# The linear attention's branch product: four dense products beside the gates, or two wide seven-product groups ahead of them

## The chip, the cores and the metric

One core of one Trainium2 chip runs the whole layer. The metric is the device time of one execution in microseconds (us), the median of three runs. A core has five engines that run their own instruction lists in order and wait for one another by semaphores: TensorE (PE in the profile; PEld is its weight load), VectorE (DVE), ScalarE (ACT), GpSimd (POOL) and SyncE (SP). In this kernel SP issues the loads from memory, and POOL issues transfers that add in flight and the writes of intermediate results.

## The reference

One decoder layer on 256 tokens of width 2048, all in float32. What matters here is the merge of three mixers:

```python
y_gla = (o_gla * jax.nn.silu(gr)) @ w_br_gla[l]      # (256, 1024) @ (1024, 2048)
y_sb  = stick_breaking_mixer(...) @ w_br_sb[l]
y_mem = memory_mixer(...) @ w_br_mem[l]
g = jax.nn.sigmoid(gates.reshape(B, T, N_BRANCH, D)) # gates = h @ W_in's last 6144 columns
merged = g[:, :, 0] * y_gla + g[:, :, 1] * y_sb + g[:, :, 2] * y_mem
x = x + merged @ w_o[l]
```

After it comes a SwiGLU feed-forward part. `y_gla` is the branch product of the title.

## The kernel before

Every weight matrix is read from memory once, in tiles `raw` of 128 partitions by 4 by 512 (1 MB): four blocks of 128 rows of the contraction and one block of 512 columns. TensorE multiplies pairs of numbers: each float32 operand is split into a high part (`wh`, made by ACT, L151) and a low part (`wl` = `raw` - `wh`, made by DVE, L152), and a product is three matmuls, high by high, high by low and low by high. The split goes in halves of 128x1024, two row blocks each. The tiles for `wh` and `wl` form a ring of five halves, so ACT and DVE can be at most five halves ahead of TensorE. A matmul has a 128x128 block of activations as weights and streams 512 columns into one PSUM bank; the 256 tokens are two blocks `t`.

There are two ways to multiply.

- `gemm` (L224 to L226): the dense product of one block of 512 columns, with two accumulators. Every half feeds 12 matmuls. The branch products and the first projections use it.
- `sgemm` (L269 to L272): two column blocks at once, a "wide group", in which part of the contraction goes by Winograd's form of Strassen's scheme, seven block products instead of eight. The blocks are two token blocks, two column blocks and two halves of the contraction, `p` row blocks long. The products are called p1 to p7 (L329 to L368: `p1`, `p2`, `p3`, `q4`, `p5`, `p6`, `p7`); a half of a product feeds 6 matmuls. p3, p5, p6 and p7 need sums of activations, the "forms" (tiles `s` before; `make_forms` makes them on DVE and ACT, L413). p5 and p6 need sums of weights: DVE adds `raw` tiles (L284). Two more sums of weights are made by transfers of POOL that add in flight (L332 and L352). What Strassen's scheme leaves over is multiplied densely by `rest`, 12 matmuls a half. DVE (L317) and ACT (L315, L346) move sums between PSUM banks and SBUF pieces `cv`. A product's second token block is added at its end by DVE (L409).

Small work such as transposes (L460), forms and merges is put in a list `background` of generators; `step()` runs one piece of it after each half, and `flush()` runs all. Behind the Python order stands a scheduler that moves instructions of each engine ahead by its own estimate, so the final order on each engine is not that of the code.

The part in question: the gates are 6144 columns, 2048 for each branch. A loop over `b` in (2, 1, 0) makes two wide groups for each branch. For `b` = 2 and 1 the sigmoid (ACT, L1078) is merged with the branch product in the background: for `b` = 1 the product was written to memory (`ysd`) and is read back as `yr`. Each merge of a column block and token block is a multiplication (L1057) and an addition (L1058). For `b` = 0, after each wide group of gates, two dense products with `w_br_gla` follow, and DVE takes them from PSUM (L1090, L1091). When four merged column blocks are there, they are transposed into chunks for the next product with `w_o`, whose forms are made during the last two dense products.

```python
        for n0 in range(0, D, 2 * NB):       # b == 0: two wide groups of gates
            ...
            if n0 > 0:
                sm_ = make_forms(tm[:1], form_tiles())
            for n, g in zip((n0, n0 + NB), gs):
                y = gemm(xo, a["w_br_gla"], n)
```

## Time and profile before

| | |
|---|---|
| time, median of 3 runs (lowest to highest) | 1609.48 us (1608.88 to 1610.42) |
| the profiled execution: time, span of its instructions | 1609.76 us, 1608.0 us |
| granted TensorE clock in it | 1.000 |
| instructions in the trace | 19432 |
| bytes moved by DMA | 395.76 MB, mean 246 GB/s |

The page gives, engine by engine, the time in which it was busy and its share of the span. A matmul's end is modelled and matmuls overlap in the records (one lasts about 0.39 us there, and the next starts sooner), so a busy TensorE says little by itself; the number of matmuls in a stretch says how fast it went.

In the profiled execution the two wide groups of gates for `b` = 1 end at about 701.2 us, and the next wide group begins there. From there to about 828.7 us stand the gates of `b` = 0 and the four dense products; the product with `w_o` follows.

### The profile page before, as it was taken

To read this page: it belongs to the slowest core of one execution; us is meant where nothing else is said; L and a number is where in the kernel's file an instruction comes from. 1 tells how busy PE (TensorE), PEld (TensorE's weight loads), DVE (VectorE), ACT (ScalarE), POOL (GpSimd) and SP (SyncE) were. 2 spreads that over 40 slices of the span, in tenths; PEclk is the share of its full clock that TensorE was granted. 3 is DMA by queue.
4 is the path that set the end of the run, shared out by engine and by line. 5 is a ranking of instruction groups with operands and counts; after the bars stand their busy time and mean duration, and the time that the engine had idled before them with its cause. 6 is when DMAs were issued, how large, how long until landed. Compare 5 with 4: busy or idle time off the path is not lost.

```text
span 1608.0 us, 19432 instructions
## 1 busy us (share of the span) xinstructions
PE 1600.8 (100%) x7198; PEld 1314.4 (82%) x7198; DVE 1361.7 (85%) x1555; ACT 1048.6 (65%) x1281; POOL 74.9 (5%) x97
## 2 busy tenths in 40 slices
PE   9999999999999999999999999999999999999998
PEld 7888888888788888888888888888888888888887
DVE  6788788887677788987799998988878989888996
ACT  7666677776666666665656766666666666666663
POOL 0000000000000000000000000000010000110000
PEclk9999999999999999999999999999999999999999
DMA  9766768667555888888757868777898686897694
GB/s 381 287 230 213 242 216 261 214 180 254 193 183 179 289 263 255 278 280 289 235 187 259 277 224 256 253 255 236 262 281 259 215 272 232 256 277 244 200 327 153
DMA packets 66672, 395.76 MB, mean 246 GB/s; under 512 B 7377, under 2 KB 14161, under 8 KB 21649
## 3 DMA queue, kind: packets, MB, share of 16 engines
q1 hardware_dynamic: 50928, 322.92, 52.5%
q0 software_dynamic: 12080, 68.16, 22.2%
q10 hardware_dynamic: 3568, 3.44, 0.7%
q8 instruction: 56, 0.92, 0.2%
q14 instruction: 40, 0.32, 0.1%
HBM read 324.24 MB, written 12.58 MB: 209 GB/s over the span
## 4 chain that ended last, share of the span: by engine, by line
PE 98%; DMA 1%; ACT 0%; DVE 0%; issue 0%; ACTq 0%; DVEq 0%
PE acc L269 20%; PE acc L272 20%; PE acc L271 20%; PE tmp L272 7%; PE tmp L269 7%; PE tmp L271 7%; PE acc L225 4%; PE acc L226 4%; PE acc L224 4%; PE tmp L460 2%; DMA raw<-in_w_br_mem 0%; PE tmp L701 0%; PE tmp L729 0%; DMA xraw<-in_memT 0%; PE tmp L817 0%; PE tmp L826 0%
## 5 line engine op out<-in xcount | busy, mean ns | idle before, releaser
L152 DVE TENSOR_TENSOR wl<-raw,wh 128x1024 fp32r<-128x1024 f32 (+1 forms) x768 | 923.9, 1222 | 204.3 <-ACT wh L151 190.3
L151 ACT CAST wh<-raw 128x1024 fp32r<-128x1024 f32 (+1 forms) x769 | 801.7, 1053 | 443.5 <-PE acc L272 238.7
L269 PE MATMUL acc<-wh,xTh 128*128 128x512 f32 x532 | 210.7, 396 | 0.2 <-ACT acc L315 0.2
L271 PE MATMUL acc<-wl,xTh 128*128 128x512 f32 x532 | 207.5, 390 | 0.0
L272 PE MATMUL acc<-wh,xTl 128*128 128x512 f32 x532 | 207.3, 390 | 0.0
L269 PE MATMUL acc<-wh,hh 128*128 128x512 f32 x452 | 178.8, 396 | 0.0
L271 PE MATMUL acc<-wl,hh 128*128 128x512 f32 x452 | 176.0, 389 | 0.0
L272 PE MATMUL acc<-wh,hl 128*128 128x512 f32 x452 | 175.0, 390 | 0.0
L284 DVE TENSOR_TENSOR raw<-raw 128x1024 f32<-128x1024 f32 x134 | 162.6, 1222 | 2.3 <-DMA raw<-in_w_gate 1.7
L224 PE MATMUL acc<-wh,oh 128*128 128x512 f32 x320 | 126.8, 398 | 0.6 <-ACT wh L151 0.6
L225 PE MATMUL acc<-wl,oh 128*128 128x512 f32 x320 | 126.0, 394 | 0.3 <-DVE wl L152 0.3
L226 PE MATMUL acc<-wh,ol 128*128 128x512 f32 x320 | 125.6, 393 | 0.0
L269 PEld LDWEIGHTS acc<-wh,xTh 128*128 128x128 f32 x532 | 99.9, 188 | 23.1 <-ACT acc L315 3.3
L269 PE MATMUL tmp<-wh,sh 128*128 128x512 f32 x300 | 118.0, 393 | 0.0
L272 PE MATMUL tmp<-wh,sl 128*128 128x512 f32 x300 | 117.1, 390 | 0.0
L272 PEld LDWEIGHTS acc<-wh,xTl 128*128 128x128 f32 x532 | 99.9, 188 | 21.0
L271 PE MATMUL tmp<-wl,sh 128*128 128x512 f32 x300 | 117.0, 390 | 0.0
L271 PEld LDWEIGHTS acc<-wl,xTh 128*128 128x128 f32 x532 | 100.0, 188 | 19.8 <-DVE wl L152 0.2
L269 PEld LDWEIGHTS acc<-wh,hh 128*128 128x128 f32 x452 | 84.8, 188 | 18.5 <-ACT acc L315 1.0
L272 PEld LDWEIGHTS acc<-wh,hl 128*128 128x128 f32 x452 | 84.8, 188 | 18.0
L271 PEld LDWEIGHTS acc<-wl,hh 128*128 128x128 f32 x452 | 85.0, 188 | 16.7
L269 PE MATMUL acc<-wh,fh 128*128 128x512 f32 x220 | 86.3, 394 | 0.0
(305 smaller groups left out, 2232.3 us busy)
## 6 DMA issues: line engine op xcount, KB each, us to landing
raw<-in_w_gate_up SPq DMA_DIRECT2D x88, 1024.0 KB, 6.8
raw<-in_w_in SPq DMA_DIRECT2D x56, 1024.0 KB, 6.2
raw<-raw POOLq DMA_DIRECT2D x53, 1024.0 KB, 7.9
raw<-in_w_gate SPq DMA_DIRECT2D x48, 1024.0 KB, 7.0
raw<-in_w_down SPq DMA_DIRECT2D x44, 1024.0 KB, 7.2
raw<-in_w_o SPq DMA_DIRECT2D x16, 1024.0 KB, 5.8
raw<-in_w_mem_kv SPq DMA_DIRECT2D x14, 1024.0 KB, 9.8
raw<-in_w_br_mem SPq DMA_DIRECT2D x8, 1024.0 KB, 5.3
```

The costliest lines, as they stand in the source:

```text
L151: act.copy(hi, src)
L152: dve.tensor_tensor(lo, src, hi.bitcast(F32), op=ALU.subtract)
L224: pe.matmul(o[t][:], xh[:, s], wh[:, j], start=k == 0, stop=False)
L225: pe.matmul(o[t][:], xh[:, s], wl[:, j], start=False, stop=False)
L226: pe.matmul(o[t][:], xl[:, s], wh[:, j], start=False, stop=k == nk - 1)
L269: pe.matmul(dst[:], xh, wh, start=id(dst) not in begun, stop=False, skip_group_check=True)
L271: pe.matmul(dst[:], xh, wl, start=False, stop=False, skip_group_check=True)
L272: pe.matmul(dst[:], xl, wh, start=False, stop=last, skip_group_check=True)
L284: dve.tensor_tensor(x, x, y, op=ALU.add)
L460: pe.transpose(dst, src, ident)
```

## The change

The product with `w_br_gla` is no longer dense and no longer follows the gates of `b` = 0. Ahead of them it is made in two wide groups of `sgemm` with `p` = 2: of the eight row blocks four go by the seven products, and four are left to `rest`. `make_forms` gets a `p`, so that its sums have two row blocks and not four; its result goes into two free chunk tiles (`outT()`, so in the trace and the order these forms are called `oh` and `ol`). Each result is copied by ACT into a piece `cv`, and POOL writes it to a new tensor in memory, `ygd`. The gates of `b` = 0 then read it back as `yr`, as those of `b` = 1 read `ysd`, and merge from SBUF. The forms for `w_o` are put in the background after the last gates. The lines of the changed program are one higher in the loop's start and four higher after it.

```diff
-    def make_forms(parts, place):
+    def make_forms(parts, place, p=SP):
...
-                        lo, hi = max(k * SP, n), min((k + 1) * SP, n + m)
+                        lo, hi = max(k * SP, n), min(k * SP + p, n + m)
...
-            a11, a12, a21, a22 = a[0, 0], a[0, 1], a[1, 0], a[1, 1]
+            a11, a12, a21, a22 = (a[at][:, :p] for at in ((0, 0), (0, 1), (1, 0), (1, 1)))
...
-                split(place[0][:, f], place[1][:, f], dst)
+                split(place[0][:, f, :p], place[1][:, f, :p], dst)
...
     ysd = dram.tile([P, 2, D], F32, name="ysd")
+    ygd = dram.tile([P, 2, D], F32, name="ygd")
...
         if b == 0:
             flush()
-            xo = pairs(o_gla)
+            sg = [x[:].rearrange("p c (f t) -> p (c f t)", t=P) for x in outT()]
+            sg = make_forms([o_gla], [x.rearrange("p (f k t) -> p f k t", f=4, k=SP) for x in sg], 2)
+            flush()
+            for n0 in range(0, D, 2 * NB):
+                for j, result in sgemm(pairs(o_gla), sg, a["w_br_gla"], (n0 // NB, n0 // NB + 1), 2):
+                    for t in range(2):
+                        v = piece()
+                        act.copy(v[:], result(t))
+                        nc.gpsimd.dma_start(ygd[:, t, n0 + j * NB : n0 + (j + 1) * NB], v[:])
         for n0 in range(0, D, 2 * NB):
             yr = []
-            if b == 1:
+            if b < 2:
                 for n in (n0, n0 + NB):
                     yr.append(gog.tile([P, 2, NB], F32, name="yr", tag="g_og"))
-                    nc.sync.dma_start(yr[-1][:], ysd[:, :, n : n + NB])
+                    nc.sync.dma_start(yr[-1][:], (ysd if b else ygd)[:, :, n : n + NB])
...
-            if n0 > 0:
-                sm_ = make_forms(tm[:1], form_tiles())
-            for n, g in zip((n0, n0 + NB), gs):
-                y = gemm(xo, a["w_br_gla"], n)
-                for t in range(2):
-                    m = merged[:, t, n : n + NB]
-                    dve.tensor_tensor(g[t], y[t][:], g[t], op=ALU.mult)
-                    dve.tensor_tensor(m, m, g[t], op=ALU.add)
+                    else:
+                        dve.tensor_tensor(g, yr[j][:, t], g, op=ALU.mult)
+                        dve.tensor_tensor(m, m, g, op=ALU.add)
...
-    background[:0] = later_on
+    sm_ = make_forms(tm[:1], form_tiles())
```

First place, DVE where the last gates of `b` = 1 end. A row `wl<-raw,wh` is a half's low part; L284 adds weights for p5 or p6; L409 is the end of the gates' second token block, and `cv<-yr,cv` with `merged<-merged,cv` are the merges of `b` = 1. Before:

```order
L152 TENSOR_TENSOR wl<-raw,wh 128x1024
L1057 TENSOR_TENSOR cv<-yr,cv 128x512
L409 TENSOR_TENSOR cv<-acc,cv 128x512
L1058 TENSOR_TENSOR merged<-merged,cv 128x512
L1057 TENSOR_TENSOR cv<-yr,cv 128x512 x2
L1058 TENSOR_TENSOR merged<-merged,cv 128x512 x2
L152 TENSOR_TENSOR wl<-raw,wh 128x1024 x2
L284 TENSOR_TENSOR raw<-raw 128x1024 x2
```

In the changed kernel, on the same engine at the same place:

```order
L1058 TENSOR_TENSOR cv<-yr,cv 128x512 x2
L1059 TENSOR_TENSOR merged<-merged,cv 128x512 x2
L423 TENSOR_TENSOR cv<-oh,ol 128x256 x4
L284 TENSOR_TENSOR raw<-raw 128x1024
L423 TENSOR_TENSOR cv<-cv 128x256
L152 TENSOR_TENSOR wl<-raw,wh 128x1024
L423 TENSOR_TENSOR cv<-cv 128x256
L152 TENSOR_TENSOR ol<-cv,oh 128x256
L423 TENSOR_TENSOR cv<-cv 128x256
L152 TENSOR_TENSOR ol<-cv,oh 128x256
L423 TENSOR_TENSOR cv<-cv 128x256
L152 TENSOR_TENSOR ol<-cv,oh 128x256
```

Up to the merges the two lists are alike; behind them stood the halves of the next gates, and now the forms of the wide group (L423 and the `ol` rows), which stand ahead of most of its halves.

The same place on TensorE. Before, from the last matmul of the gates' p1 on (`sh` is a form of the gates, `xTh` the tokens themselves):

```order
L272 MATMUL tmp<-wh,xTl 128x512
L269 MATMUL tmp<-wh,sh 128x512
L269 MATMUL acc<-wh,xTh 128x512
L271 MATMUL acc<-wl,xTh 128x512
```

In the changed kernel, from the last matmul of the dense rest that follows p1: two single matmuls that belong to later halves, then p5, whose activations are the new forms:

```order
L272 MATMUL acc<-wh,ol 128x512
L269 MATMUL acc<-wh,oh 128x512 x2
L269 MATMUL tmp<-wh,oh 128x512
L271 MATMUL tmp<-wl,oh 128x512
L272 MATMUL tmp<-wh,ol 128x512
```

p5 now comes 18 matmuls and those two after the group's start; in the kernel before, the gates' forms at this place had long been made.

Second place, ACT. Before, at the end of the gates of `b` = 0 and the start of the first dense product:

```order
L1078 ACTIVATE cv<-acc,r_x 128x512
L151 CAST wh<-raw 128x1024
L1078 ACTIVATE cv<-cv,r_x 128x512
L151 CAST wh<-raw 128x1024 x6
```

In the changed kernel, at the end of the first wide group with `w_br_gla` and the start of the second (L315 and L346 carry sums out of PSUM bank `tmp`, L1075 copies results for memory):

```order
L315 COPY cv<-tmp 128x512
L1075 COPY cv<-acc 128x512
L315 COPY acc<-tmp 128x512
L1075 COPY cv<-cv 128x512
L1075 COPY cv<-acc 128x512
L1075 COPY cv<-cv 128x512
L151 CAST wh<-raw 128x1024 x3
L346 COPY cv<-tmp 128x512
```

These copies are new, and they stand ahead of the high parts of the second group's p6 and later halves; the dense products before had none.

Third place, DVE in the first wide group of `w_o`. `cv<-oh,ol` and `cv<-cv` of 128x512 are the forms of `w_o`, `sl<-cv,sh` their low parts. Before, where p5 of that group begins:

```order
L152 TENSOR_TENSOR ol<-tmp,oh 128x512
L152 TENSOR_TENSOR wl<-raw,wh 128x1024 x3
L152 TENSOR_TENSOR ol<-tmp,oh 128x512
L284 TENSOR_TENSOR raw<-raw 128x1024 x2
L152 TENSOR_TENSOR ol<-tmp,oh 128x512
L152 TENSOR_TENSOR wl<-raw,wh 128x1024
```

In the changed kernel:

```order
L423 TENSOR_TENSOR cv<-oh,ol 128x512
L284 TENSOR_TENSOR raw<-raw 128x1024
L423 TENSOR_TENSOR cv<-cv 128x512
L284 TENSOR_TENSOR raw<-raw 128x1024
L152 TENSOR_TENSOR sl<-cv,sh 128x512
L423 TENSOR_TENSOR cv<-cv 128x512
L152 TENSOR_TENSOR wl<-raw,wh 128x1024
L423 TENSOR_TENSOR cv<-cv 128x512
L152 TENSOR_TENSOR sl<-cv,sh 128x512
```

The twelve rows of forms stood among the halves of the last two dense products, between 807 and 829 us; now they stand among the halves of `w_o` itself, next to the sums of weights of its p5.

## The prediction

> **What bounds the kernel now.** I read the page first (engines, then the TensorE clock), then stretches of time around the change, then groups of instructions for durations, then single rows at the place where the new work goes in. The page:

> ```profile
> PE 1600.8 (100%) x7198; PEld 1314.4 (82%) x7198; DVE 1361.7 (85%) x1555; ACT 1048.6 (65%) x1281; POOL 74.9 (5%) x97
> PEclk9999999999999999999999999999999999999999
> ```

> TensorE is never without a matmul and has its full clock. Whether that is its speed or a slow feed is told by how many it begins in a stretch. The table by stretch (columns: engine, busy us, number of instructions):

> ```profile
> 640.00:720.00 80.00, 80.00 (x353) 65.56 (x352) 71.87 (x74) 51.84 (x57) 2.58 (x3) 1.00 0.87 282
> 742.00:764.00 22.00, 22.00 (x102) 18.20 (x101) 15.81 (x17) 10.54 (x13) 0.86 (x1) 1.00 0.63 226
> 807.00:829.00 22.00, 22.00 (x99) 18.22 (x98) 21.68 (x29) 11.52 (x15) 0.00 (x0) 1.00 0.49 171
> ```

> In the gates (first row) 353 matmuls begin in 80 us, one in 0.227 us. DVE is busy 71.87 of 80 us there, so it has little room; in the first dense product (second row) 15.81 of 22. TensorE bounds, and DVE follows close behind. How close is seen where the gates of the second branch end. TensorE, then DVE:

> ```profile
> 701.21 0.39 PE L269 MATMUL tmp<-wh,xTh 128*128 128x512 f32 x1
> ...
> 711.05 0.41 PE L269 MATMUL acc<-wh,xTh 128*128 128x512 f32 x1
> 711.30 0.47 PE L271 MATMUL tmp<-wl,sh 128*128 128x512 f32 x1
> 711.61 0.39 PE L272 MATMUL tmp<-wh,sl 128*128 128x512 f32 x1
> ```

> ```profile
> 701.17 0.69 DVE L1057 TENSOR_TENSOR cv<-yr,cv 128x512 f32<-128x512 f32 x1
> 701.77 0.69 DVE L409 TENSOR_TENSOR cv<-acc,cv 128x512 f32<-128x512 f32 x1
> 702.37 0.69 DVE L1058 TENSOR_TENSOR merged<-merged,cv 128x512 f32<-128x512 f32 x1
> 702.97 1.29 DVE L1057 TENSOR_TENSOR cv<-yr,cv 128x512 f32<-128x512 f32 x2
> 704.17 1.29 DVE L1058 TENSOR_TENSOR merged<-merged,cv 128x512 f32<-128x512 f32 x2
> 705.38 2.36 DVE L152 TENSOR_TENSOR wl<-raw,wh 128x1024 fp32r<-128x1024 f32 x2
> 707.64 2.36 DVE L284 TENSOR_TENSOR raw<-raw 128x1024 f32<-128x1024 f32 x2
> 710.00 4.63 DVE L152 TENSOR_TENSOR wl<-raw,wh 128x1024 fp32r<-128x1024 f32 x4
> ```

> The new wide group begins at 701.21; call that S. DVE has no gap from there to 714: end of the last gates, merges, two halves, weight sums, halves. The first half in the last row ends 1.22 us after 710.00, at 711.22, and the matmul that needs it begins at 711.30 and not 0.23 us after 711.05. So at this boundary DVE's lead over TensorE is used up to the last tenth, and any work added to DVE here is paid by TensorE. Here the change adds work. The rows also give DVE's step in a full queue: 0.60 us for 128x512 (701.77 to 702.37), 1.14 for 128x1024 (two rows from 705.38, the next at 707.64).

> **The change, part by part.** Durations of one instruction (mean ns behind the busy time), and below them a run of four casts on ACT and the transposes of the stretch 742 to 764:

> ```profile
> L152 DVE TENSOR_TENSOR wl<-raw,wh 128x1024 fp32r<-128x1024 f32 x766 | 922.5, 1223 | 204.2 <-ACT wh L151 190.3 <-PE tmp L460 2.0 <-ACT cr L605 0.3
> L809 DVE TENSOR_TENSOR rb<-rb,cst 128x256 f32<-128x256 f32 x8 | 3.3, 418 | 0.0
> L151 ACT CAST wh<-raw 128x1024 fp32r<-128x1024 f32 x766 | 800.1, 1055 | 443.5 <-PE acc L272 238.7 <-PE acc L226 63.9 <-DVE raw L284 41.3
> L154 ACT ACTIVATE hh<-tmp,vecs 128x256 fp32r<-128x256 f32 x16 | 7.4, 473 | 3.2 <-DVE hl L155 1.7 <-PE tmp L460 1.5
> L346 ACT COPY cv<-tmp 128x512 f32<-128x512 f32 x25 | 14.6, 586 | 5.5 <-PE tmp L272 5.1
> ...
> 708.91 3.91 ACT L151 CAST wh<-raw 128x1024 fp32r<-128x1024 f32 x4 [4.15 <-DVE raw L284]
> ...
> L460 PE MATMUL tmp<-cst,merged 128*128 128x128 f32 x8 | 1.2, 272 | 0.0
> ```

> A 128x256 addition has 0.418 us; less the 0.09 by which a 128x512 overlaps the next (0.69 against 0.60), its step is 0.33. ACT's casts step by 0.98 (four in 3.91 us), its copies by about 0.55.

> *Matmuls removed.* A dense product has 8 row blocks x 2 x 3 = 48 matmuls, four of them 192. A wide group with two of four row blocks by seven has 7 products x 6 = 42, and 4 halves of rest x 12 = 48, so 90; two groups 180. Twelve fewer at 0.227 us: **-2.7 us**. Transposes stay 16 on each side. The dense stage is no slower per matmul than the gates: its row has 102 instructions in 22 us, 8 of them transposes that step by 0.11 (four in 0.44, below): 94 x 0.227 + 0.9 = 22.2.

> *DVE and ACT in sum.* DVE gets 6 halves and 4 weight sums of 128x1024, 12 operations of 128x256 for the forms and 8 more of 128x512: 10 x 1.14 + 12 x 0.33 + 8 x 0.60 = 20.2 us. ACT gets 6 casts, 14 copies and 4 small casts: 6 x 0.98 + 14 x 0.55 + 4 x 0.4 = 15 us. Spread evenly up to the end of w_o's first group both would hide; what counts is where they stand.

> *The forms of the first wide group.* The state at S is that of the trace, since the two programs are alike up to there. DVE is through the merges at 705.38, S + 4.17. Then the order gives four additions (to 5.49), a weight sum (6.63), an addition (6.96), a half (8.10), an addition (8.43), and the low part of p5's forms, done at 8.85. The cast of its high part waits on ACT behind p6's own high part, which waits for that weight sum: about 8.25. TensorE has from S only p1 (6 matmuls), the dense rest (12), two strays and, with the high form, two of p5: 22 x 0.227 = 4.99 us. The third of p5 needs the low part: at 8.9, **3.9 us of idle**. Behind that, two additions and two more low parts bring p6's half to start at 10.08 and end at 11.30; TensorE would be there at 10.03: **1.3 more**. Sum +5.2. Bounds: 3.9 if p6's half comes in time; 6.0 if a 128x256 steps by its whole 0.418 (nine of them x 0.09). I take 5.2, as the steps come from a full queue at this very place. Behind the stalled TensorE, ACT and DVE get back their lead.

> *The copies at the second group.* p1 there ends 1.4 us after the group's start; then ACT copies four sums of 128x512 (0.55 each) before it casts p6's high part, so p6's low part is there at about 6.0 us, and TensorE is there at 25 x 0.227 = 5.7. Three more casts and a copy follow before the stray of the second dense rest, which costs about 0.9. Together **+1.3**, bounds 0 and 2.5. The upper end is a late weight load:

> ```profile
> raw<-raw POOLq DMA_DIRECT2D x4, 512.0 KB, 6.8
> ysd<-cv POOLq DMA_DIRECT2D x2, 256.0 KB, 10.3
> yr<-ysd SPq DMA_DIRECT2D x4, 512.0 KB, 6.4
> ```

> SP is in order, and the next gates' first load waits for a tile that POOL's adding transfer still reads; the third weight tile of this group is queued behind it. In the sum above it is in time by about a microsecond.

> *ygd.* Eight writes on POOL, four reads on SP. The first four go out a few us into the second group and take 10.3; their reader is first needed a whole group later (20 us and more). Two loads of gates go ahead of the reads on SP. On POOL the writes stand ahead of the second group's adding transfer, which waits for later work anyway. Taken as 0; if that cover were gone, the reads' 6.4 us would delay the gates' loads, which are 1 MB tiles loaded well ahead.

> *Merges of the first third.* Their number is unchanged, now from SBUF like those of L1057. Between the two groups of gates stand 4 low parts of transposes more than in the rows above, 2.4 us of DVE, against 16 transposes of TensorE, four of which take

> ```profile
> 831.63 0.44 PE tmp L460 x4
> ```

> so 1.76 us. The bound is 0 to 0.6; the order puts them between halves that the dense rest covers, so 0.

> *The forms of w_o.* Before, they lay in the last dense product, in the gaps that halves of 12 matmuls leave:

> ```profile
> L423 DVE TENSOR_TENSOR cv<-oh,ol 128x512 f32<-128x512 f32 x4 | 2.5, 688 | 0.0
> L152 DVE TENSOR_TENSOR sl<-cv,sh 128x512 fp32r<-128x512 f32 x4 | 2.7, 687 | 0.0
> ```

> Now DVE has, from the start of w_o (where it stands as at S, at its first merge) to the half of p6: 23 operations of 128x512 and 13 of 128x1024, 13.8 + 14.8 = 28.6 us, then that half 1.2: ready at 29.9 with the small overlap. TensorE's way there is 110 matmuls and 16 transposes, 24.97 + 1.76 = 26.7. **+3.2**; bounds 0 (a lead that I don't see) and 4.3 (the same lag again where the group ends, L409 and the transposes of x2).

> **Sum.** -2.7 + 5.2 + 1.3 + 3.2 = +7.0. The profiled execution took 1609.76 us (span 1608.0), 0.28 above the median of the runs, so 1609.48 + 7.0 = **1616.5 us**.

> **The rivals.** *All hidden.* The forms come in time, and only the matmuls count: 1609.5 - 2.7 = 1606.8. It needs DVE's chain from S to the low form to fit in 5.0 us and not 8.9; it would if the six operations at 701.17 to 705.38 were done before S. Against it: two of them need the last gates' sums, and the rows have them after S. *First stall alone.* w_o and the copies are covered by leads of some us: 1609.5 - 2.7 + 5.2 = 1612.0. For it: ACT and DVE may lead by five halves, and where these feed 12 matmuls each, as in w_o's rest, that is 13.6 us. *Faster.* All hidden, and small waits of the kernel before go as well, such as 0.1 at 711 and 0.27 in the row below (two matmuls, 0.72 and not 0.45): 1609.5 - 3.1 = 1606.4, and a little more of the kind passes the limit.

> ```profile
> 768.30 0.72 PE acc L269 x2
> ```

> *A late load.* The third weight tile of the second group comes a whole landing of 6.8 us late in place of the 1.3: 1622.0. *DVE is the bound.* Then twelve matmuls are worth nothing, and DVE's 20.2 us are paid in full: 1629.7. Against it: 0.227 us in every stretch, at DVE shares from 72% (15.81 of 22) to 99%. [...]

> **How the numbers follow.** About 0.2%, 3.2 us, can be told from no change here: below 1606.3 is faster, above 1612.7 slower. Chances: forecast 0.62 (its own range 1613 to 1620), first stall alone 0.15, all hidden 0.12, faster 0.04, late load 0.04, DVE the bound 0.03. So faster 0.04; same 0.15 + 0.12 = 0.27; slower 0.62 + 0.04 + 0.03 = 0.69. Low end: -2.7 + 3.9 = 1610.7; high end: -2.7 + 6.0 + 2.5 + 4.3 = 1619.6. The range is 1610.5 to 1620.

> **What would show it.** Twelve matmuls fewer, at 0.227 us elsewhere. A gap of TensorE of 3 to 5 us some 5 us after the first wide group begins, ended by DVE's `ol` or ACT's `oh`, and a shorter one at p6's half. Shorter gaps at the second group, ended by ACT's `wh`, and in w_o about 22 to 27 us after its start, ended by DVE's `wl`. DVE without a gap over both. No wait on `yr`. The prediction is wrong if TensorE's largest gap lies elsewhere, above all before a weight load, or if w_o runs without one.

## The result and the profile after

The changed kernel takes 1623.13 us (median of five runs, 1621.65 to 1625.82), the kernel before 1609.48: ratio 1.0083, 95% interval 1.0073 to 1.0094, that is 13.65 us slower. The forecast was 1616.5, with a range to 1620.0. The profiled execution took 1622.01 us, 12.25 above that of before. First its page and the table by stretch; the stretches are the two wide groups with `w_br_gla`, the gates of `b` = 0, and `w_o`:

```profile
PE 1604.6 (99%) x7186; PEld 1311.7 (81%) x7186; DVE 1380.2 (85%) x1585; ACT 1060.2 (65%) x1305; POOL 82.6 (5%) x109
```

```profile
701.00:749.00 48.00, 44.66 (x181) 34.04 (x180) 39.11 (x48) 30.60 (x38) 4.81 (x7) 0.96 0.70 220
749.00:836.00 87.00, 84.68 (x378) 68.88 (x377) 77.50 (x79) 57.31 (x67) 5.66 (x8) 1.00 0.87 289
836.00:927.00 91.00, 87.90 (x393) 69.92 (x392) 87.14 (x100) 58.69 (x78) 5.43 (x8) 1.00 0.76 248
```

The page says next to nothing: 3.8 us more of busy TensorE, its share from 100% to 99%. The table says where: TensorE is idle 3.3 us in the first stretch, 2.3 in the second and 3.1 in the third, and the first has a granted clock of 0.96. What each group costs is told by its first matmuls on TensorE's timeline: first group of `w_br_gla`, second, gates, second group of gates, `w_o`, feed-forward part.

```profile
700.69 0.39 PE L269 MATMUL tmp<-wh,oh 128*128 128x512 f32 x1
...
727.23 0.39 PE L269 MATMUL tmp<-wh,oh 128*128 128x512 f32 x1
...
748.80 0.39 PE L269 MATMUL tmp<-wh,xTh 128*128 128x512 f32 x1
...
792.78 0.39 PE L269 MATMUL tmp<-wh,xTh 128*128 128x512 f32 x1
...
835.62 0.39 PE L269 MATMUL tmp<-wh,oh 128*128 128x512 f32 x1
...
926.83 0.39 PE L269 MATMUL tmp<-wh,hh 128*128 128x512 f32 x1
```

So the lengths are 26.5, 21.6, 44.0, 42.8 and 91.2 us. Matmuls alone (0.227 each, a transpose 0.11, as in the kernel before) would take 20.4, 20.4, 40.9, 42.6 and 85.2. In the kernel before, the first group of these gates took 41.0 (701.21 to 742.25), gates and dense products together 127.5, `w_o` 85.6. Up to `w_o` that is 134.9 against 127.5, +7.4; `w_o` +5.6; the parts before and behind it -0.8: 12.25. Four groups lose time, and TensorE's rows show what each waits for.

**First group.** TensorE, and DVE at the same time:

```profile
705.42 0.40 PE L269 MATMUL acc<-wh,oh 128*128 128x512 f32 x1
706.77 0.50 PE L269 MATMUL acc<-wh,oh 128*128 128x512 f32 x1 [0.95 <-ACT wh L151]
708.86 0.50 PE L269 MATMUL tmp<-wh,oh 128*128 128x512 f32 x1 [1.58 <-ACT oh L151]
...
711.02 0.63 PE L272 MATMUL tmp<-wh,ol 128*128 128x512 f32 x1
711.45 0.63 PE L269 MATMUL tmp<-wh,oh 128*128 128x512 f32 x1
712.10 0.80 PE L271 MATMUL tmp<-wl,oh 128*128 128x512 f32 x1
```

```profile
704.86 1.43 DVE L423 TENSOR_TENSOR cv<-oh,ol 128x256 f32<-128x256 f32 x4
706.20 1.22 DVE L284 TENSOR_TENSOR raw<-raw 128x1024 f32<-128x1024 f32 x1
707.34 0.42 DVE L423 TENSOR_TENSOR cv<-cv 128x256 f32<-128x256 f32 x1
707.67 1.22 DVE L152 TENSOR_TENSOR wl<-raw,wh 128x1024 fp32r<-128x1024 f32 x1
```

Between 705.42 and 708.86 TensorE begins one matmul. The forms (L423) stand on DVE as the order had them, ahead of most sums and halves, and p5 starts (708.86) when its form's high part is there. Then something else happens: after 709.6 a matmul begins about every 0.43 us and not every 0.227. The table in steps of 2 us shows it in the granted clock (the number behind POOL's):

```profile
706.00:708.00 2.00, 0.50 (x1) 0.19 (x1) 2.00 (x4) 1.27 (x2) 0.00 (x0) 1.00 0.00 0
708.00:710.00 2.00, 1.12 (x3) 0.68 (x4) 2.00 (x5) 1.28 (x4) 0.00 (x0) 0.92 0.00 0
710.00:712.00 2.00, 2.00 (x5) 1.08 (x4) 2.00 (x5) 1.05 (x3) 0.00 (x0) 0.50 0.00 0
712.00:714.00 2.00, 1.99 (x7) 1.58 (x7) 1.51 (x3) 1.22 (x2) 0.00 (x0) 0.73 0.00 0
```

If it is half wherever it is not full, it was half for 2 x (0.16 + 1.00 + 0.54) = 3.4 us, from 709.7 to 713.1. The last row shown of TensorE, at 712.10, is p6's first matmul with a low part.

**Second group.** A shorter wait for ACT, behind its copies, as foreseen:

```profile
735.27 0.73 PE L269 MATMUL acc<-wh,oh 128*128 128x512 f32 x2 [0.39 <-ACT wh L151]
```

**First gates.** Timelines of TensorE, DVE and SP, and SP's wait for the write of `ygd` (in total, times, longest):

```profile
752.68 0.50 PE L269 MATMUL tmp<-wh,sh 128*128 128x512 f32 x1 [1.00 <-ACT wh L151]
754.45 0.50 PE L271 MATMUL acc<-wl,xTh 128*128 128x512 f32 x1 [1.04 <-DVE wl L152]
```

```profile
750.25 1.23 DVE L284 TENSOR_TENSOR raw<-raw 128x1024 f32<-128x1024 f32 x1 [4.37 <-DMA raw<-in_w_gate]
...
787.53 0.69 DVE L1094 TENSOR_TENSOR cv<-yr,cv 128x512 f32<-128x512 f32 x1
```

```profile
721.05 0.33 SPq L263 DMA_DIRECT2D raw<-in_w_gate  x1
737.72 1.68 SPq L1082 DMA_DIRECT2D yr<-ygd  x2
740.72 15.18 SPq L263 DMA_DIRECT2D raw<-in_w_gate  x5
```

```profile
SPq L1082 <- DMA ygd<-cv: 16.3, 1, 16.3
```

DVE stands idle 4.37 us for a weight tile. That tile was issued behind 740.72, because SP stood from 721.4 to 737.7 at the read of `yr`, which waited for the write of `ygd` to land; DVE first uses `yr` at 787.5, 50 us later.

**w_o.** TensorE waits for DVE's low parts and then for ACT's high part, whose sum of weights stands on DVE behind the forms:

```profile
859.64 0.50 PE L271 MATMUL tmp<-wl,sh 128*128 128x512 f32 x1 [0.72 <-DVE wl L152]
861.38 0.50 PE L271 MATMUL acc<-wl,oh 128*128 128x512 f32 x1 [0.31 <-DVE wl L152]
865.73 0.50 PE L269 MATMUL acc<-wh,sh 128*128 128x512 f32 x1 [1.56 <-ACT wh L151]
...
887.47 0.50 PE L271 MATMUL acc<-wl,oh 128*128 128x512 f32 x1 [0.32 <-DVE wl L152]
...
892.93 0.50 PE L269 MATMUL tmp<-wh,sh 128*128 128x512 f32 x1 [0.18 <-ACT wh L151]
```

```profile
858.37 1.22 DVE L152 TENSOR_TENSOR wl<-raw,wh 128x1024 fp32r<-128x1024 f32 x1
859.51 0.69 DVE L152 TENSOR_TENSOR sl<-cv,sh 128x512 fp32r<-128x512 f32 x1
860.11 1.22 DVE L152 TENSOR_TENSOR wl<-raw,wh 128x1024 fp32r<-128x1024 f32 x1
861.24 3.49 DVE L284 TENSOR_TENSOR raw<-raw 128x1024 f32<-128x1024 f32 x3
864.65 4.63 DVE L152 TENSOR_TENSOR wl<-raw,wh 128x1024 fp32r<-128x1024 f32 x4
```

The loss does not end with these gaps: the 120 matmuls and 16 transposes from 865.73 to 897.11 take 31.4 us, where they alone would take 29.0. DVE is busy 87.14 of 91 us in `w_o`; before it was 77.09 of 85:

```profile
829.00:914.00 85.00, 85.00 (x391) 70.19 (x390) 77.09 (x83) 57.00 (x72) 5.44 (x8) 1.00 0.78 256
```

### The profile page after: what moved, and what is told of

It is laid out like the page before. It is cut to its first block, busy times and chain, and to the rows that moved or that the text cites. A ratio compares the mean times of both kernels' runs of the same rounds, so it can differ in the third digit from the quotient of the medians.

```text
span 1620.2 us, 19488 instructions
## 1 busy us (share of the span) xinstructions
PE 1604.6 (99%) x7186; PEld 1311.7 (81%) x7186; DVE 1380.2 (85%) x1585; ACT 1060.2 (65%) x1305; POOL 82.6 (5%) x109
## 4 chain that ended last, share of the span: by engine, by line
PE 94%; DVE 3%; DMA 1%; ACT 1%; issue 0%; ACTq 0%; DVEq 0%; SPq 0%
PE acc L269 20%; PE acc L271 19%; PE acc L272 19%; PE tmp L272 7%; PE tmp L271 7%; PE tmp L269 7%; PE acc L225 4%; PE acc L226 4%; PE acc L224 4%; PE tmp L460 2%; DVE wl L152 1%; ACT wh L151 1%; DMA raw<-in_w_gate 1%; DVE raw L284 1%; DMA raw<-in_w_br_mem 0%
## 5 line engine op out<-in xcount | busy, mean ns | idle before, releaser
L152 DVE TENSOR_TENSOR wl<-raw,wh 128x1024 fp32r<-128x1024 f32 (+1 forms) x774 | 929.1, 1220 | 192.8 <-ACT wh L151 179.8
L151 ACT CAST wh<-raw 128x1024 fp32r<-128x1024 f32 (+1 forms) x775 | 804.6, 1051 | 426.2 <-PE acc L272 231.7
L269 PE MATMUL acc<-wh,xTh 128*128 128x512 f32 x532 | 210.5, 396 | 0.5 <-ACT acc L315 0.4
L271 PE MATMUL acc<-wl,xTh 128*128 128x512 f32 x532 | 207.6, 390 | 1.0 <-DVE wl L152 1.0
L272 PE MATMUL acc<-wh,xTl 128*128 128x512 f32 x532 | 207.4, 391 | 0.0
L269 PE MATMUL acc<-wh,hh 128*128 128x512 f32 x452 | 178.7, 396 | 0.0
L271 PE MATMUL acc<-wl,hh 128*128 128x512 f32 x452 | 176.1, 390 | 0.0
L272 PE MATMUL acc<-wh,hl 128*128 128x512 f32 x452 | 175.4, 390 | 0.0
L284 DVE TENSOR_TENSOR raw<-raw 128x1024 f32<-128x1024 f32 x138 | 167.1, 1219 | 6.7 <-DMA raw<-in_w_gate 6.0
L269 PE MATMUL tmp<-wh,sh 128*128 128x512 f32 x300 | 118.4, 395 | 1.2 <-ACT wh L151 1.2
L269 PEld LDWEIGHTS acc<-wh,xTh 128*128 128x128 f32 x532 | 99.9, 188 | 23.4 <-ACT acc L315 3.7
L271 PE MATMUL tmp<-wl,sh 128*128 128x512 f32 x300 | 117.1, 390 | 0.7 <-DVE wl L152 0.7
L272 PE MATMUL tmp<-wh,sl 128*128 128x512 f32 x300 | 117.2, 391 | 0.0
L271 PEld LDWEIGHTS acc<-wl,xTh 128*128 128x128 f32 x532 | 100.0, 188 | 21.2 <-DVE wl L152 1.5
L272 PEld LDWEIGHTS acc<-wh,xTl 128*128 128x128 f32 x532 | 99.9, 188 | 20.9
L224 PE MATMUL acc<-wh,oh 128*128 128x512 f32 x256 | 101.6, 400 | 0.6 <-ACT wh L151 0.6
L225 PE MATMUL acc<-wl,oh 128*128 128x512 f32 x256 | 100.9, 394 | 0.1
L226 PE MATMUL acc<-wh,ol 128*128 128x512 f32 x256 | 100.5, 393 | 0.0
L269 PEld LDWEIGHTS acc<-wh,hh 128*128 128x128 f32 x452 | 84.9, 188 | 18.4 <-ACT acc L315 1.0
L272 PEld LDWEIGHTS acc<-wh,hl 128*128 128x128 f32 x452 | 84.8, 188 | 18.0
L271 PEld LDWEIGHTS acc<-wl,hh 128*128 128x128 f32 x452 | 85.0, 188 | 17.0 <-DVE wl L152 0.3
L269 PE MATMUL acc<-wh,fh 128*128 128x512 f32 x220 | 86.3, 394 | 0.0
```

The lines of the kernel that those rows point to most:

```text
L151: act.copy(hi, src)
L152: dve.tensor_tensor(lo, src, hi.bitcast(F32), op=ALU.subtract)
L224: pe.matmul(o[t][:], xh[:, s], wh[:, j], start=k == 0, stop=False)
L225: pe.matmul(o[t][:], xh[:, s], wl[:, j], start=False, stop=False)
L226: pe.matmul(o[t][:], xl[:, s], wh[:, j], start=False, stop=k == nk - 1)
L269: pe.matmul(dst[:], xh, wh, start=id(dst) not in begun, stop=False, skip_group_check=True)
```

## The experiments

The theory: four separate waits, each paid by TensorE at its own place, and their prices add. The rivals: DVE's work in sum is the bound, so moving it gains nothing; the seven products are all of the loss; the stalls hide each other. For each kernel the group lengths of its profiled execution are read as above.

| kernel | median, us | group 1 | group 2 | gates 1 | gates 2 | w_o |
|---|---|---|---|---|---|---|
| changed | 1623.13 | 26.5 | 21.6 | 44.0 | 42.8 | 91.2 |
| forms early | 1616.86 | 22.4 | 21.6 | 42.9 | 42.8 | 91.2 |
| read late | 1619.99 | 26.3 | 21.6 | 41.5 | 42.8 | 91.2 |
| forms of `w_o` left out | 1616.93 | 26.1 | 21.6 | 47.1 | 42.8 | 85.6 |
| both moves | 1615.27 | 22.4 | 21.6 | 41.6 | 42.8 | 91.2 |
| filled gap (12 matmuls more) | 1624.92 | 26.1 | 21.6 | 45.7 | 42.8 | 91.2 |
| three repaired | 1610.43 | 22.4 | 21.6 | 41.7 | 42.9 | 85.7 |

**Forms early.** The forms of `w_br_gla` are made right behind the activations that they are built from.

```diff
     background.append(gla_T())
+    sg = ... outT() ...
+    sg = make_forms([o_gla], ..., 2)
...
-            sg = ... outT() ...
-            sg = make_forms([o_gla], ..., 2)
```

> The forms of the product w_br_gla are made in the background right after the activations they are built from, while the gates of b = 2 and b = 1 run, and not at the start of the first wide group. Nothing is left out. Theory A (four separate waits, each paid by TensorE at its own place): the two gaps of TensorE at 705 to 709 us and the half clock behind them go, 6.1 us of excess in that group; the other three places stay. 1623.1 - 6 = about 1617. Rival B (DVE has too much work in sum, 85% of the span and about 90% in the gates): what is taken from this place is paid in the gates, no change, 1622 to 1624. Rival C (only the wait, 4.4 us, goes, because the clock falls at another place): about 1618.7.

1616.86 us, ratio 1.0045 (1.0033 to 1.0058). The first group is 4.2 us shorter, at full clock, and the gates 1.1. DVE had room for the forms in the earlier gates, so its sum of work is not the bound. What is left in the first group, 1.9 us over its matmuls, comes from p6's sum of weights, which stands on DVE behind the six merges.

**Read late.** `yr` for the first gates is first touched by ACT after their p5, so that SP has the read behind the weight tiles.

```diff
-                    nc.sync.dma_start(yr[-1][:], ...)
+                    if b or n0:
+                        nc.sync.dma_start(yr[-1][:], ...)
...
+            def read(x, yr=yr):            # called after p5 of the first gates
+                for n, v in zip((0, NB), yr):
+                    act.copy(v[:, 0, :1], x[:, :1])
+                    nc.sync.dma_start(v[:], ygd[:, :, n : n + NB])
```

> The first two reads of the product from memory (yr for the first third of the gates) are made to wait for the end of p5 of those gates (ACT writes one column of the tile first), so that SP has them behind six weight tiles of the gates and not ahead of them. Nothing is left out. Theory A: SP stood 16.3 us at these reads, waiting for a write to land; with them behind, the gates' third tile lands before DVE wants it, and the 2.9 us of excess at 751 to 755 us go: about 1620.2. Rival D (that tile is late for another reason, because its buffer comes free late after POOL's adding transfer): no change, 1623.

1619.99 us, ratio 1.0068 (1.0054 to 1.0082). The same rows of SP and DVE:

```profile
721.57 38.95 SPq L263 DMA_DIRECT2D raw<-in_w_gate  x7
761.71 1.63 SPq L1091 DMA_DIRECT2D yr<-ygd  x2
```

```profile
748.07 1.22 DVE L284 TENSOR_TENSOR raw<-raw 128x1024 f32<-128x1024 f32 x1 [1.92 <-DMA raw<-in_w_gate]
```

The read itself cost nothing; the tiles behind it did. The gates are 2.5 us shorter.

**Forms of w_o left out.** The products with `w_o` take the gates' forms in place of their own: the same number of matmuls, but the output is wrong, and the work of DVE and ACT on these forms is not done.

```diff
-    sm_ = make_forms(tm[:1], form_tiles())
+    sm_ = sx
```

> The forms of w_o are left out: its products take the forms of the gates in their place (wrong numbers in the output, the same matmuls), so DVE and ACT have 12 and 4 operations of 128x512 less in the first wide group of w_o. Theory A: the 3.1 us of excess at 858 to 866 us go and most of the 2.0 at 885 to 895 with it: 1618 to 1619. Rival B (the first group of w_o is short of DVE also without forms, by its sums of weights, merges and transposes): 1 us or less is gained, 1622.

1616.93 us, ratio 1.0044 (1.0032 to 1.0057), 6.2 below the changed kernel where 4 to 5 were expected. `w_o` takes 85.6, exactly as in the kernel before:

```profile
838.00:924.00 86.00, 86.00 (x395) 70.80 (x394) 80.92 (x90) 58.33 (x77) 5.90 (x9) 1.00 0.82 268
```

**Dense ahead.** The dense products at the new place, through memory.

```diff
-                for j, result in sgemm(pairs(o_gla), sg, a["w_br_gla"], ..., 2):
+            for n in range(0, D, NB):
+                y = gemm(pairs(o_gla), a["w_br_gla"], n)
```

> The product w_br_gla is made ahead of the gates of b = 0 and goes through memory as in the changed kernel, but dense, in four products of 48 matmuls; no seven products, no forms for it, no sums of weights. Nothing is left out. Theory A: +2.7 for twelve matmuls, -6.1 - 1.1 without forms and copies in the way; the late tile and the stall of w_o stay (2.9 + 5.1 over the kernel before): about 1617 to 1618. Rival E (the seven-product form is all of the loss): 1609.5 to 1611, as the kernel before.

1615.89 us, ratio 1.0039 (1.0026 to 1.0051): 7.2 below the changed kernel, with twelve matmuls more. The product takes 43.5 us at the changed kernel's place (two wide groups: 48.1), and TensorE has no gap in it nor in the gates, 83.7 us:

```profile
700.00:744.00 44.00, 44.00 (x196) 36.45 (x195) 26.28 (x26) 21.93 (x26) 4.75 (x8) 1.00 0.77 266
744.00:827.00 83.00, 83.00 (x375) 68.23 (x374) 70.57 (x71) 54.93 (x61) 3.18 (x5) 1.00 0.81 260
```

So one expectation was wrong: the late tile did not stay. SP waits for the writes of `ygd` here too, 14.3 us, but in three parts and earlier, as the dense product is done column block by column block:

```profile
SPq L1079 <- DMA ygd<-cv: 14.3, 3, 6.8
```

The tile behind the second read is issued at 730.4 and not after 740.7, and DVE does not wait for it. What is left over the kernel before, 6.4 us, is in `w_o`, 92.3 against 85.6; the other 7.2 of the loss go with the two wide groups at that place.

**Both moves.** Forms early and read late together.

> The two moves together: forms of w_br_gla made early, and the first two reads of the product behind six weight tiles of the gates on SP. Nothing is left out. Theory A (the places are separate, so their prices add): 1623.1 - 6.3 - 3.1 = 1613.7. Rival F (the stalls hide each other: what one place gives back is lost at the next): 1616 to 1617, no better than the forms alone.

1615.27 us, ratio 1.0036 (1.0023 to 1.0049). 7.9 of the 9.4 us of the single moves, so 1.6 less than expected. The gates explain 1.1 of the difference: with the forms early they had already gained that much.

**Filled gap.** Twelve useless matmuls in the changed kernel's first group.

```diff
         def p5():
+            z = tmp()
+            for _ in range(fill):
+                pe.matmul(z[:], xs[0][0][:, :P], o_gla[0][:, :2]..., start=True, stop=True)
```

> The changed kernel with twelve more matmuls of 128x512 in the first wide group of w_br_gla, three behind p1 and nine right ahead of p5, into a PSUM bank that nobody reads: work for nothing, in the time in which TensorE waits for the forms. Theory G (the half clock from 709.6 to 713.1 us is TensorE's answer to having begun 2 matmuls in 3.8 us, and it costs what lies behind p6's wait, about 0.9 us): the clock stays full there, 1622.2, and the times of the five runs lie closer together, as they do in the runs without that gap. Rival H (the clock falls for another reason, at a time or with the load of all engines): the same dip and the same or a longer time, 1623 to 1626; twelve matmuls paid in full would be 1625.8.

1624.92 us (1624.43 to 1625.35), ratio 1.0096 (1.0082 to 1.0109): the clock stays full in the first group, as expected, and the runs lie closer together, but the time is 1.8 us longer and not 0.9 shorter. The first group has 12 matmuls more and takes 26.1 us, less than without them, at full clock. But the half clock is now at the gates, which wait for the late tile:

```profile
708.00:710.00 2.00, 1.47 (x8) 0.89 (x6) 2.00 (x4) 1.40 (x3) 0.00 (x0) 1.00 0.00 0
710.00:712.00 2.00, 1.98 (x7) 1.08 (x7) 2.00 (x7) 1.15 (x4) 0.00 (x0) 1.00 0.00 0
...
756.00:758.00 2.00, 1.76 (x5) 1.27 (x5) 2.00 (x3) 1.36 (x2) 0.84 (x2) 0.50 0.83 279
758.00:760.00 2.00, 2.00 (x8) 1.58 (x7) 2.00 (x3) 1.05 (x1) 0.90 (x1) 0.65 0.84 207
```

```profile
753.66 0.50 PE L269 MATMUL tmp<-wh,sh 128*128 128x512 f32 x1 [1.38 <-ACT wh L151]
```

So the half clock came behind a stall each time, and which of two stalls it strikes differs. Its price is the part that no other wait covers. In the first group p6's first matmul with a low part begins 11.4 us after the group's start in four kernels: the changed one, read late, forms of `w_o` left out, and this one. In the first three the half clock lasts 1.0, 0.6 and 0.0 us beyond that matmul, and the groups take 26.5, 26.3 and 26.1 us; without it here, 26.1. At the gates it costs more. They take 45.7 us against 44.0; 0.4 of that is a longer wait for the tile (the row above, 1.38 where the changed kernel has 1.00), and about 1.4 is left for the half clock. The kernel without forms for `w_o` had it at both places, with 47.1 us in the gates, of which 1.6 over the changed kernel is a longer wait (2.65 us at the same matmul), in its profiled execution, the slowest of its five (1618.8). TensorE was not without work ahead of a fall: in the 3.4 us ahead of the fall at 709.7 in the changed kernel four matmuls began (706.77, 708.86, 709.20 and 709.62), and four ahead of that at 756.0 here (753.66, 753.99, 755.43 and 755.77). At the changed kernel's gates no more than four began in as long a stretch, from 751.4 to 754.8 (752.68, 753.01, 754.45 and 754.79), and the clock stayed at 1.00. What decides whether a stall brings the half clock is not shown.

**Sum by POOL, and merges later.** Two attempts at a faster version, on top of both moves: in the first group of `w_o` the sum for q4 by POOL's adding transfer, and, in the second kernel, the last merges of `b` = 1 between the halves of the first wide group.

```diff
-            if moved and not late:                                  # in p2: q[11] += q[21] by POOL
+            if moved and (not late or late == "sum"):
...
-            flush()                                                 # second kernel: ahead of w_br_gla
```

> The two moves together, and in the first wide group of w_o the sum of weights for q4 is made by POOL's adding transfer and not by two additions of DVE (one of which stands right ahead of p6's halves there). Nothing is left out. Theory A (that group waits for DVE, whose queue is full of forms): DVE is 1.1 us earlier at p6 and 2.3 in all, 1613.7 - 1 to 2.3 = 1611.4 to 1612.7. Rival J (the wait there is for the weight tile, or moves to the transfer): 1613.7 or more.

> As the one before (two moves, sum by POOL), and the last merges of b = 1 are not all put ahead of the first wide group of w_br_gla: they go in the background between its halves. Nothing is left out. Theory A: of the 1.9 us at p6 of that group, which is what is left there with the forms early (706 to 708.5), one or so goes, as DVE has the sum of weights and a half ahead of one merge: 1 below the kernel before it, 1610.5 to 1611.7. Rival J: no difference to it.

1613.05 us (1.0023, 1.0014 to 1.0032) and 1613.01 (1.0022, 1.0012 to 1.0031). Unlike what the expectations say, the numbers change: POOL takes the sum before p5 and p6 have changed its operand, so q4 has other weights in both, and their output is wrong. The first is 2.2 us below both moves, the gain that was expected, from a base 1.6 above the one that was expected. `w_o` is 2.0 us shorter (89.2), as two additions of DVE go. The merges shorten the first group by 1.6 us (20.8) and lengthen the second by 0.8 and the gates by 0.3, and the time does not move, where 1 us less was expected.

**Three repaired.** Forms early, read late, and the forms of `w_o` left out, all at once; like the kernel that leaves these forms out alone, it does less work and its output is wrong.

> Forms of w_br_gla early, its first reads late, and the forms of w_o left out (its products take the gates' forms; wrong numbers in the output, the same matmuls): all three waits of the changed kernel taken away at once. Theory A (prices add): 1615.3 - 5.6 = 1609.7, the time of the kernel before; the twelve matmuls saved are then still eaten inside the two wide groups, where 43.96 us stand against 43.5 for the dense products. Rival K (the seven-product form pays once the waits are gone): 1606.8 or less. Rival F (the stalls hide each other): 1612 or more.

1610.43 us, ratio 1.0004 (0.9995 to 1.0013): the time of the kernel before; 1609.7 was expected. The three single gains add up to 15.6 us (6.3, 3.1 and 6.2) and together give 12.7, so the prices do not quite add. The twelve matmuls do not come out as a gain even then: product and gates take 128.5 us, against 127.5 before and 127.2 for dense ahead. 2.7 us of matmuls are saved, and 1.9, 1.1 and 0.8 are lost at p6, behind the copies and at the gates.

**Forms of w_o late, alone.** One part of the change in the kernel before, in two measurements; the trace is from the second.

```diff
-            if n0 > 0:
-                sm_ = make_forms(tm[:1], form_tiles())
...
     background[:0] = later_on
+    sm_ = make_forms(tm[:1], form_tiles())
```

> The kernel before with one part of the change alone: the forms of w_o are put in the background after the last gates and products, as in the changed kernel, and not ahead of the last two dense products. Nothing is left out. Theory A1 (these 12 additions and low parts cost what they cost wherever the first group of w_o has to hold them): 1609.5 + 5.6 = about 1615. Theory A2 (they cost because in the changed kernel gates stand ahead of w_o, which leave DVE no lead, and here dense products stand there, in which it can run ahead): 1610.5 to 1612. Rival (other work moved with them is the cause): 1609.5.

> The kernel before with the forms of w_o late once more, for its trace: the product with w_o takes 85.6 us in the kernel before and 91.2 in the changed one. Theory A2 (2.3 us for the forms, the rest for the gates ahead of it): about 88 us here, with one gap of TensorE at p6 of its first group and none at the start of its second. Theory A1: 90 or more.

1611.92 us, ratio 1.0014 (1.0005 to 1.0023), and 1611.5 in the single run, beside 1608.6 of the kernel before. `w_o` takes 87.4 us there (828.43 to 915.78). The one gap is not where I had put it, but in the second group:

```profile
889.92 0.39 PE L269 MATMUL tmp<-wh,sh 128*128 128x512 f32 x1
891.39 0.50 PE L269 MATMUL acc<-wh,oh 128*128 128x512 f32 x1 [1.09 <-ACT wh L151]
```

So `w_o` takes 85.6 us with neither, 85.6 with gates ahead and no forms in it, 87.4 with forms and dense products ahead, 91.2 with both. Neither alone explains it: the forms are dear because gates stand ahead.

## Why the prediction was wrong, step by step

- *Matmuls, -2.7*: right, in count (7186 against 7198) and price.
- *First group, +5.2*: right in place and mechanism, a little small. p5's low part is first used 8.5 us after the start and p6's 11.4, where 8.9 and 11.3 were worked out. 26.5 - 20.4 = 6.1 us, of which 0.5 is the half clock, which no row of the kernel before could show beside such a gap. It came as two waits (0.95 and 1.58 us, first for a high part, then for `oh`), and p6's wait lies under the half clock.
- *Second group, +1.3*: 21.6 - 20.4 = 1.1, ended by ACT's `wh`, right.
- *ygd, 0*: the step that failed first. I had SP's order and counted two loads of gates ahead of the reads, but costed only the reads' own landing, and looked for who needs `yr`. The price lay in what stands behind them: SP waits in order for the write of `ygd`, and the gates' third tile stands behind it. 44.0 against 41.0 us, +2.9, of which the late read gives back 2.5. The rival of a late load had the mechanism, with the wrong tile and a chance of 0.04.
- *Gates between the groups, 0*: right, 42.8 against 42.6 of matmuls.
- *w_o, +3.2*: the step that failed by size. The gaps at p5 and p6 are there, 24 to 30 us after the start, and p6's half begins 30.1 us after it, where 29.9 was worked out. But I ended the count at p6, as if DVE caught up behind it, and the bound of 4.3 allowed only 1.1 more. It does not catch up: TensorE loses some 2.4 us more up to 897, where x2's sums and transposes come. +5.6.
- *The median*: the forecast went from one execution to the median by 0.28. Here the median lies 1.1 above the profiled execution. That this is the half clock at other places in other runs fits the filled gap, and the runs without the first group's gap (1616.66 to 1617.53 with the forms early); it is not shown for these runs. The mean granted clock that is kept of each run goes with the time in read late (1619.02 to 1619.99 us at 0.999, 1620.88 and 1622.67 at 0.998), but in the changed kernel the fastest run, 1621.65, has 0.998 too, and the profiled one 0.999.

So 7.0 + 2.9 + 2.4 + 0.9 - 0.2 = 13.0, less the 0.8 that the parts before and behind gained, is the 12.25 of the profiled execution. *DVE is the bound* was the rival closest on the far side, 1629.7: DVE's added work was indeed paid at the boundaries, but work moved to an earlier place came for nothing (forms early).

## What to carry to other kernels

Before a read-back is put on an in-order load queue, ask what stands behind it and when the write before it lands, not when its reader needs it: here a read that nobody needed for 50 us cost 2.5. Where a second engine is as busy as DVE is here (85% of the span), a step moved off a place where it has slack can be paid for beyond the first wait (here 5.6 us in `w_o`, where 3.2 were worked out up to it); count to the end of the next product. Saved matmuls are worth only what the other engines can follow: twelve fewer came with 18.5 us more of busy DVE in the page (1380.2 against 1361.7) and gave nothing even with the three waits taken away (1610.43 us against 1609.48).
